# DeltaNet trunk: pair products at fixed places in the z quarters, earlier adds of a v half, and more weight buffers with a fixed load order in the memory product

## The chip, the cores and the metric

The kernel runs on one core of one Trainium2 chip. The metric is the device time of one execution in microseconds (us). Every time below is of the kernel before the change: three timed runs, and one profiled execution whose trace is quoted.

## What is computed

A decoder trunk of two layers on 256 tokens of width 2048, in fp32. Layer 0 mixes tokens with an mLSTM, layer 1 with a gated DeltaNet. Each layer then attends to 256 memory tokens and applies a squared-ReLU MLP. Keys and values of the memory are computed once, ahead of everything. Cut to what the change touches:

```python
def rms_norm(x, g):
    y = x * rsqrt(mean(x * x, -1) + EPS)
    return y * g

kv = rms_norm(mem, mem_norm_g) @ w_mem_kv              # the memory product: k_m and v_m
...
def mlstm_mixer(h, w_in, ...):                         # layer 0
    q, k, v, o, ig, fg = split(h @ w_in)
...
def gdn_mixer(h, w_in, ...):                           # layer 1
    qkv, z, bt, a = split(h @ w_in)
    q, k, v = split(silu(causal_dwconv(qkv, conv_w)))
    q = l2_norm(q) * GD_K ** -0.5                      # 16 heads of 128
    k = l2_norm(k)
    g = -exp(a_log) * softplus(a + dt_bias)            # decays, 32 heads
    gam = cumsum(g)
    A   = (k * beta) @ k.T * exp(gam_i - gam_j)        # strictly lower, by chunks of 64
    Aqk = q @ k.T * exp(gam_i - gam_j)
    ...
    return (rms_norm(o) * silu(z)) @ w_out
```

## The kernel before

**Weights.** Every product streams its fp32 weights once from memory. A unit of 1 MB comes as two halves of 512 KB, each by one DMA that SP issues (L149) into one of four `raw` buffers. ACT rounds a half to a high part (`hi`, the CAST of L169) and DVE subtracts that from the raw to get a low part (`lo`, L170). There are three hi and three lo buffers. TensorE (PE) forms a product as high by high, low by high and high by low: three matmuls. `take` hands out the next unit and begins the loads of the units after it. All engines run their instructions in order, and so does each engine's DMA queue; the order itself is laid out ahead of time by a scheduler that ranks the instructions by priority and by its own durations. `behind(a, b)` puts an instruction after another in that order, without a wait on the chip.

**The memory product.** For each of four chunks of mem, PE transposes the chunk (`mtp`, L896) and ACT and DVE split it; k_m (L438) and then v_m (L534 to L536) follow, with one unit of weights for each 512 rows. Beside v_m, `x_chunk(c)` prepares x: `load_x(c)` loads a chunk as two pieces, PE transposes them (`ltp`, L310), ACT and DVE write them as `h` (L349, L350). `load_x` holds a load back by a MEMSET of one element, which stands behind the split of a certain half (the list `splits`). All of it is loaded by SP's queue.

**The mLSTM's q, k and v.** Units f = 4 to 15 of q and k alternate with parts of v. v is formed in two halves by sums of seven products, in seven banks. When a half is complete, `keep_v` lets ACT copy the banks out (L1009), and seven additions put them together: for the second half on DVE, for the first by POOL's accumulating DMAs (L1060), one behind each f, two behind f = 11. Then come the output gate o (L450, L456) and the heads, whose first products are `sp` (L1085).

**The DeltaNet's quarters.** For each quarter c of the heads: four units of q (`gq`), four of k (`gk`), in the first quarter also the gates (`ab`, `suf`), then the z product `gz` (L534 to L536) of four units by two halves of the tokens, which makes eight slots of twelve matmuls. After a convolution (`conv`: DVE, ACT) q and k of a head are one tile `gqk`. `norms(c)` squares the four tiles on ACT (`l2sq`, L1682), sums them on PE (`l`, L1686) and forms `rk`, `nrk` and `bq` on ACT and DVE. `decays(grp)` forms the decays `gdm`: twelve small DVE instructions (L1651, L1653) from rows `grow` that POOL loads by DMA, and two Exp on ACT (L1654). `pairs(grp)` forms for two heads the products `g` on PE (L1703, L1704), scales them out of the banks as `gm` (DVE L1705 and L1707, ACT L1709) and multiplies them by the decays (`at`, L1713), which POOL stores. These are written before and behind `early_z(c)`, and the scheduler is free to place them. The small products take turns in three banks (`psum`).

Of the kernel before, what the change touches and what calls it, by code (L numbers as in the profile page):

```python
# [7 lines left out]
F32 = mybir.dt.float32  # L8
# [29 lines left out]
class Weights:  # L38


    def __init__(self, tc, ctx, ahead, bufs):
# [5 lines left out]
        self.first, self.splits, self.n_pair = 0, None, 0  # L47
# [16 lines left out]
    def after(self, load):  # L64


        self.tc.add_manual_dep(load.ins, self.last.ins.name, mybir.DependencyInfo(
            mybir.DependencyClass.NoSync, mybir.DependencyReason.DATA), reason="issue order")
        self.last = load
# [51 lines left out]
    def begin(self, place=None):  # L121
# [25 lines left out]
        for k0 in range(0, kb, hb):  # L147
            raw = self.raw.tile([P, hb, un], F32, tag="raw", name=f"raw{i}_{k0}")
            self.last = nc.sync.dma_start(raw[:, :, :n], src[k0 * P : (k0 + hb) * P, :].rearrange("(kb p) n -> p kb n", p=P))  # L149
# [27 lines left out]
    def prefetch(self, n):  # L177
        while self.done < min(len(self.plan), self.taken + n):
            for half in self.begin():

                with self.tc.high_priority(offset=self.first):
                    ins = half()
                if self.splits is not None and ins:
                    self.splits.append(ins[1])
# [11 lines left out]
def trunk(ctx: ExitStack, tc, x, mem, norm_g, mem_norm_g, w_mem_kv, w_xq, w_xo, w_up, w_down,  # L196
# [272 lines left out]
    def prod_tall(key, srcs, n_fb, evac, ahead=None, then=None, wide=False):  # L469

        for f in range(n_fb):
            hi, lo, nk, n = ws.take(key, ahead)
            a = acc(f"{key}{f}")
            for k in range(nk):
# [9 lines left out]
                m = PE.matmul(a[:, 0:T], lo[k], srcs[k][:, 0:T], start=False, stop=(k == nk - 1))  # L484
            evac(f, Bank(a, wide))
# [24 lines left out]
    def prod_tok(key, srcs, n_ch, evac, after=None, post=None, start=None, free=None, split=False):  # L510
# [37 lines left out]
        for p_ in pairs:  # L548
# [22 lines left out]
            for t in range(2):  # L571
                for i in p_:
# [4 lines left out]
                    else:  # L577
                        run(i, t)
                    done(i, t)
# [247 lines left out]
    kv = kv_stack.enter_context(tc.tile_pool(name="kv", bufs=1))  # L827
    kmT = kv.tile([P, XA_H, T], F32, name="kmT")
# [4 lines left out]
    def load(dst, src, c):  # L833
        return nc.sync.dma_start(dst[c], src[0, :, c * 512 : (c + 1) * 512].rearrange("(t p) d -> p t d", p=P))
# [50 lines left out]
    def load_x(c):  # L885

        behind(V.memset(xk[c][:1, 0, 0:1], 0.0), splits[2 * c + 5])
        for t in range(2):
            nc.sync.dma_start(xk[c][:, t, :], x[0, t * P : (t + 1) * P, c * 512 : (c + 1) * 512])

    def mem_chunk(c, other=None):
# [8 lines left out]
        for i in range(4):  # L900
            k = c * 4 + i
            chain(*split_into(mh[k], banks[i % 2][:, i // 2 * T : (i // 2 + 1) * T], cols[:, COL_MEM + k : COL_MEM + k + 1]))
            if i % 2:
                chain(*first.pop(0)())
                splits.append(last[1])
# [12 lines left out]
    splits = []  # L918
    ws.splits = splits
# [57 lines left out]
    kv_stack.close()  # L977

# [8 lines left out]
    def mlstm(sc, h, rms, before):  # L987
# [61 lines left out]
        for f in range(4, KB):  # L1049
# [7 lines left out]
            for _ in range(2 if f == 11 else 1):  # L1057
# [489 lines left out]
    def gdn(g0, lead):  # L1547
# [30 lines left out]
        def prod_v(c):  # L1578
            vts[c] = [acts.tile([P, 2, T], F32, tag=f"u{c % 2 * 2 + i}", name=f"vT{c}_{i}") for i in range(2)]
            return prod_tall("gv", h, 4, lambda f, a: conv(32 + c * 4 + f, a, vts[c][f // 2][:, f % 2, :]),  # L1580
                             wide=c not in steps)
# [13 lines left out]
        with tc.tile_pool(name="gd1", bufs=1) as sc:  # L1595
# [46 lines left out]
            def decays(grp):  # L1642
# [371 lines left out]
```

## Time and profile before

| what | value |
|---|---|
| median of 3 runs | 2815.34 us (2814.28 to 2815.68) |
| the profiled execution | 2815.06 us, of which the trace spans 2813.4 us |
| PE busy | 2778.0 us, 99% of the span |
| DVE, ACT, POOL busy | 2223.1, 1843.5, 367.8 us |
| mean granted TensorE clock | 0.995 |
| moved by DMA | 633.45 MB, mean 225 GB/s |

A wait in the profile is idle time of an engine just before an instruction, with the line that waited and the instruction that ended the wait, as far as semaphore events show it. The granted clock is the share of TensorE's full rate that it was given in a stretch; at half of it a matmul of 512 columns follows the one before by 0.43 us and not by 0.23. A timeline row reads: start, duration, engine, line, operation, output and inputs, tile, count, and in brackets the idle time ahead of it with its releaser.

### The profile page before, as it was taken

How to read it: one execution, taken by the hardware profiler on the slowest of the kernel's cores; microseconds unless marked ns; L12 is line 12 of the kernel's file. 1: busy time of each engine (PE TensorE's matmuls, PEld its weight loads, DVE VectorE, ACT ScalarE, POOL GpSimd, SP SyncE). 2: the span in 40 equal slices, each digit the busy share in tenths (PEclk: the TensorE clock that was granted, in tenths of full speed). 3: DMA queues.
4: the chain of work that ended last, by engine and by line, in shares of the span. 5: the costliest groups of instructions: out<-in, count | busy, mean ns of one | idle time of the engine just before them, and what ended most of it. 6: DMA issues, size and time to landing. Idle time of an engine off the chain costs nothing.

```text
span 2813.4 us, 42450 instructions
## 1 busy us (share of the span) xinstructions
PE 2778.0 (99%) x15552; PEld 2373.1 (84%) x15552; DVE 2223.1 (79%) x3263; ACT 1843.5 (66%) x3013; POOL 367.8 (13%) x602
## 2 busy tenths in 40 slices
PE   9999999999999999999999999999999999999998
PEld 7888888888888888887887998888888888888887
DVE  6997756788999988788776895555577789999786
ACT  6666646777778776466765554544467777778763
POOL 0110000011111110002211104231000111122100
PEclk9999999999999999999999999999999999999999
DMA  7786465689999998858877778665656899999985
GB/s 236 214 227 184 151 215 166 185 238 258 262 252 255 258 256 247 263 154 237 241 207 212 219 200 283 208 198 187 214 156 197 236 261 257 266 250 257 256 246 195
DMA packets 581488, 633.45 MB, mean 225 GB/s; under 512 B 29040, under 2 KB 431296, under 8 KB 579488
## 3 DMA queue, kind: packets, MB, share of 16 engines
q1 hardware_dynamic: 530816, 516.55, 60.2%
q0 software_dynamic: 49568, 113.10, 17.4%
q8 instruction: 122, 2.00, 0.3%
q10 hardware_dynamic: 896, 1.09, 0.1%
q14 instruction: 86, 0.70, 0.1%
HBM read 545.91 MB, written 68.22 MB: 218 GB/s over the span
## 4 chain that ended last, share of the span: by engine, by line
PE 37%; DVE 6%; DMA 4%; ACT 3%; issue 2%; POOL 0%; SPq 0%; DVEq 0%; ACTq 0%; POOLq 0%
PE up L1463 6%; PE up L1465 3%; DVE lo L170 3%; PE m L1497 2%; PE m L1498 2%; PE m L1499 2%; PE g_out L535 2%; PE g_out L536 2%; PE g_out L534 2%; DMA raw<-in_gdn_w_in 1%; PE down L535 1%; PE down L536 1%; PE down L534 1%; DVE cv L1573 1%; PE gz L534 1%
## 5 line engine op out<-in xcount | busy, mean ns | idle before, releaser
L170 DVE TENSOR_TENSOR lo<-raw,hi 128x1024 fp32r<-128x1024 f32 (+1 forms) x716 | 849.9, 1219 | 241.2 <-ACT hi L169 239.4
L169 ACT CAST hi<-raw 128x1024 fp32r<-128x1024 f32 (+1 forms) x716 | 723.4, 1048 | 354.3 <-issue 38.9
L1463 PE MATMUL up<-h,hi 128*128 128x512 f32 x1792 | 424.9, 389 | 0.9 <-ACT h_up L1291 0.9
L1463 PEld LDWEIGHTS up<-h,hi 128*128 128x128 f32 x1792 | 336.0, 188 | 72.2 <-ACT h_up L1291 2.2
L94 DVE TENSOR_TENSOR lo<-tsum,hi 128x1024 fp32r<-128x1024 f32 x208 | 247.1, 1220 | 56.5 <-ACT hi L98 40.4
L98 ACT CAST hi<-tsum 128x1024 fp32r<-128x1024 f32 x208 | 212.7, 1051 | 115.3 <-DVE tsum L94 75.2
L1465 PEld LDWEIGHTS up<-h,lo 128*128 128x128 f32 x1792 | 229.8, 191 | 8.7
L1465 PE MATMUL up<-h,lo 128*128 128x256 f32 x1792 | 232.4, 283 | 0.0
L1293 POOL DMA_DIRECT2D u<-h_up x96 | 82.8, 862 | 771.7 <-ACT h_up L1291 643.7
L94 DVE TENSOR_TENSOR lo<-rawp,hi 128x512 fp32r<-128x512 f32 (+1 forms) x160 | 150.6, 952 | 1.2 <-ACT hi L113 1.0
L1498 PE MATMUL m<-lo,s 128*128 128x512 f32 x352 | 138.5, 394 | 0.0
L1497 PE MATMUL m<-hi,s 128*128 128x512 f32 x352 | 138.4, 393 | 0.0
L1499 PE MATMUL m<-hi,s 128*128 128x512 f32 x352 | 138.1, 392 | 0.0
L1365 POOL DMA_DIRECT2D sums_d<-kept x110 | 111.0, 1111 | 147.3 <-ACT kept L1361 98.8
L535 PE MATMUL down<-lo,u 128*128 128x512 f32 x320 | 124.5, 389 | 0.0
L536 PE MATMUL down<-hi,u 128*128 128x512 f32 x320 | 124.5, 389 | 0.0
L534 PE MATMUL down<-hi,u 128*128 128x512 f32 x320 | 124.5, 389 | 0.0
L94 DVE TENSOR_TENSOR tsum<-rawp 128x1024 f32<-128x1024 f32 x80 | 97.9, 1224 | 22.4 <-DMA rawp<-in_w_down 20.6
L1573 DVE SCALAR_TENSOR_TENSOR cv<-pad,cols,cv 128x256 f32<-128x256 f32 x192 | 92.2, 481 | 16.7 <-ACT cv L1571 12.6
L1498 PE MATMUL m<-lo,u 128*128 128x512 f32 x264 | 103.9, 394 | 0.3 <-DVE lo L94 0.3
L1497 PE MATMUL m<-hi,u 128*128 128x512 f32 x264 | 103.8, 393 | 0.0
L1499 PE MATMUL m<-hi,u 128*128 128x512 f32 x264 | 103.1, 391 | 0.0
(542 smaller groups left out, 6669.4 us busy)
## 6 DMA issues: line engine op xcount, KB each, us to landing
raw<-in_w_up SPq DMA_DIRECT2D x256, 512.0 KB, 6.2
raw<-in_gdn_w_in SPq DMA_DIRECT2D x192, 512.0 KB, 5.0
rawp<-in_w_down SPq DMA_DIRECT2D x160, 512.0 KB, 6.5
raw<-in_mlstm_w_in SPq DMA_DIRECT2D x96, 512.0 KB, 4.7
raw<-in_w_down SPq DMA_DIRECT2D x96, 512.0 KB, 5.5
raw<-in_gdn_w_out SPq DMA_DIRECT2D x64, 512.0 KB, 4.8
sums_d<-kept POOLq DMA_DIRECT2D x38, 512.0 KB, 8.4
sums_d<-kept POOLq DMA_DIRECT2D x72, 256.0 KB, 7.2
```

The costliest lines, as they stand in the source:

```text
L94: sub = lambda d, a, b: nc.vector.tensor_tensor(d, a, b, ALU.subtract)
L98: nc.scalar.copy(ht[:, j : j + 2, :], t[:, j : j + 2, :])
L169: a = nc.scalar.copy(h_, raw[:, :, :n])
L170: return a, nc.vector.tensor_tensor(l_, raw[:, :, :n], h_, ALU.subtract)
L534: PE.matmul(a, sh, hi[j], start=(kk == 0), stop=False)
L535: PE.matmul(a, sh, lo[j], start=False, stop=False)
L536: end[0] = PE.matmul(a, sl, hi[j], start=False, stop=(kk == nk - 1))
L1463: PE.matmul(a, hi[k], h[k][:, :], start=(k == 0), stop=False, skip_group_check=True)
L1465: PE.matmul(a[:, T:], lo[k], h[k][:, 0:T], start=False, stop=(k == nk - 1), skip_group_check=True)
L1497: PE.matmul(a, sh, hi[i], start=(j == 0), stop=False)
L1498: PE.matmul(a, sh, lo[i], start=False, stop=False)
L1499: PE.matmul(a, sl, hi[i], start=False, stop=(j == FK // 2 - 1))
```

## The change

It has three parts.

1. **Memory product.** A second pool `wmore` of five buffers takes the halves whose running number leaves over 4 when divided by 9 (5 to 8, 14 to 17 and so on); the other halves keep the four buffers. All loads of this stage (mem, weights, x) are chained on SP in the order in which the program writes them. The MEMSETs that held the x loads back are removed. `wmore` is closed with the stage.
2. **Adds of the first v half.** `1 if f < 11 else 2`: of the seven adds one goes behind f = 10 and two each behind f = 11, 12 and 13, where before it was one behind f = 10, two behind 11, and one each behind 12 to 15.
3. **z quarters.** `norms` and `pairs` are cut into steps, and a list gives the slots of `gz` behind which a step stands. Slot 1: the first two squares. Slot 4: their sums, and the other two squares. Slot 5: their sums, with rk, nrk and bq. Slot 6: the first decays and the first pair. Slot 7: the second pair. Slot 8: the second decays and the third pair. The fourth pair stands behind the first unit of the next `gq` (or `gv`). The small matmuls are put behind the slot's last matmul, the decays on DVE behind the step before them.

```diff
@@ Weights.begin
-            raw = self.raw.tile([P, hb, un], F32, tag="raw", name=f"raw{i}_{k0}")
-            self.last = nc.sync.dma_start(raw[:, :, :n], ...)
+            self.halves += 1
+            pool = self.more if self.more and self.halves % 9 > 4 else self.raw
+            raw = pool.tile([P, hb, un], F32, tag="raw", name=f"raw{i}_{k0}")
+            d = nc.sync.dma_start(raw[:, :, :n], ...)
+            if self.more:
+                self.after(d)
+            self.last = d
@@ the memory product
+    ws.more = kv_stack.enter_context(tc.tile_pool(name="wmore", bufs=5))
...
-        return nc.sync.dma_start(dst[c], src[0, :, c * 512 : (c + 1) * 512]...)
+        ws.after(nc.sync.dma_start(dst[c], src[0, :, c * 512 : (c + 1) * 512]...))
...
-        behind(V.memset(xk[c][:1, 0, 0:1], 0.0), splits[2 * c + 5])
         for t in range(2):
-            nc.sync.dma_start(xk[c][:, t, :], ...)
+            ws.after(nc.sync.dma_start(xk[c][:, t, :], ...))
...
     kv_stack.close()
+    ws.more = None
@@ mlstm
-            for _ in range(2 if f == 11 else 1):
+            for _ in range(1 if f < 11 else 2):
@@ gdn, decays: each of the twelve
-                            V.tensor_scalar(dm[kh][:, v2, tt, :], ...)
+                            behind(V.tensor_scalar(dm[kh][:, v2, tt, :], ...), other)
@@ gdn
+            at_m, ends, l2, gdms = [], [], {}, {}
+
+            def turn(m, todo):
+                at_m[:] = [m]
+                while todo:
+                    do, *args = todo.pop(0)
+                    do(*args)
+
+            def g_mm(*a, **kw):
+                behind(PE.matmul(*a, **kw), at_m[0])
+
+            def squares_of(c, i0):
+                for i in (i0, i0 + 1):
+                    sq = l2[i] = acts.tile([P, 2, T], F32, tag=f"u{12 + i % 2}", name="l2sq")
                     S.activation(sq, qks[c][i], AF.Square)
+
+            def l2_sums(c, i0):
...
+            def decay(c, g):
+                gdms[2 * c + g] = decays(2 * c + g, ends[0]), g0.tile([P, 6, 4, P], F32, tag="at", name="at")
+
+            def pair(c, g, kh):
...
@@ early_z
-                prod_tok("gz", h, 1, ev)
+                turns = [[(squares_of, c, 0)], [], [], [(l2_sums, c, 0), (squares_of, c, 2)], [(l2_sums, c, 2)],
+                         [(decay, c, 0), (pair, c, 0, 0)], [(pair, c, 0, 1)], [(decay, c, 1), (pair, c, 1, 0)]]
+                prod_tok("gz", h, 1, ev, slot=lambda m: turn(m, turns.pop(0)))
+                later.append((pair, c, 1, 1))
...
-                norms(c)
-                pairs(c * 2)
                 early_z(c)
-                pairs(c * 2 + 1)
```

How the order moves on three engines follows, at the places of which the prediction speaks.

SP's queue near the start, before, from the fifth unit of the weights on (`raw` is a half of weights, `xs` a piece of x):

```order
L149 DMA raw_0_405<-in_w_mem_kv 128x2x512
L149 DMA raw_2_407<-in_w_mem_kv 128x2x512
L889 DMA xs_104<-in_x 128x512
L149 DMA raw_0_415<-in_w_mem_kv 128x2x512
L149 DMA raw_2_417<-in_w_mem_kv 128x2x512
L149 DMA raw_0_486<-in_w_mem_kv 128x2x512
L889 DMA xs_104<-in_x 128x512
L149 DMA raw_2_488<-in_w_mem_kv 128x2x512
L889 DMA xs_104<-in_x 128x512
L149 DMA raw_0_545<-in_w_mem_kv 128x2x512
L149 DMA raw_2_547<-in_w_mem_kv 128x2x512
```

The same stretch of the change:

```order
L152 DMA raw_0_408<-in_w_mem_kv 128x2x512
L152 DMA raw_2_410<-in_w_mem_kv 128x2x512
L152 DMA raw_0_418<-in_w_mem_kv 128x2x512
L152 DMA raw_2_420<-in_w_mem_kv 128x2x512
L897 DMA xs_104<-in_x 128x512
L897 DMA xs_105<-in_x 128x512
L152 DMA raw_0_487<-in_w_mem_kv 128x2x512
L152 DMA raw_2_489<-in_w_mem_kv 128x2x512
L897 DMA xs_104<-in_x 128x512
L897 DMA xs_105<-in_x 128x512
L152 DMA raw_0_545<-in_w_mem_kv 128x2x512
L152 DMA raw_2_547<-in_w_mem_kv 128x2x512
```

Before, four pieces of x also stood ahead of or inside the third unit of weights, and of the others some between the halves of a unit. Now the first x pieces stand behind six whole units, and from there a chunk's pieces alternate with units. `raw_0_545` is the half whose cast stands on ACT just ahead of the first `h` of x, before and now.

DVE in the first quarter, before, at the decays and the small tiles of `norms` (`bq` reads `l`):

```order
L1651 TENSOR_SCALAR gdm<-grow,cum,cml 128x128
L1653 TENSOR_SCALAR gdm<-grow,sufb 128x128
L1651 TENSOR_SCALAR gdm<-grow,cum,cml 128x128
L373 RECIPROCAL rk<-rk 128x8
L1691 TENSOR_SCALAR bq<-l_12141 128x2x4
L1690 TENSOR_SCALAR nrk<-rk 128x2x4
L1651 TENSOR_SCALAR gdm<-grow,cum,cml 128x128
L1653 TENSOR_SCALAR gdm<-grow,sufb 128x128
L1705 SCALAR_TENSOR_TENSOR gm<-g_12193,rk,masks 128x2x128
L1707 SCALAR_TENSOR_TENSOR gm<-g_12194,rk,masks 128x2x128
```

The same place in the change:

```order
L377 RECIPROCAL rk<-rk 128x8
L1715 TENSOR_SCALAR bq<-l_12215 128x2x4
L1714 TENSOR_SCALAR nrk<-rk 128x2x4
L1657 TENSOR_SCALAR gdm<-grow,cum,cml 128x128 x2
L1659 TENSOR_SCALAR gdm<-grow,sufb 128x128
L1657 TENSOR_SCALAR gdm<-grow,cum,cml 128x128
L176 TENSOR_TENSOR lo_12480<-raw_0_12475,hi_12479 128x1024
L176 TENSOR_TENSOR lo_12480<-raw_8_12477,hi_12479 128x1024
L1657 TENSOR_SCALAR gdm<-grow,cum,cml 128x128
L1659 TENSOR_SCALAR gdm<-grow,sufb 128x128
L1657 TENSOR_SCALAR gdm<-grow,cum,cml 128x128 x2
L1659 TENSOR_SCALAR gdm<-grow,sufb 128x128
```

The reciprocal, `bq` and `nrk` stood behind most decays and stand ahead of all of them now; two splits of weights have come in among the decays, and the `gm` follow three rows further on.

PE in the second quarter, before, at the first sums (`gz_0` and `gz_1` are the two halves of the tokens):

```order
L536 MATMUL gz_1_12948<-hi_12759,h_11431 128x512
L534 MATMUL gz_1_12948<-hi_12759,h_11428 128x512
L1686 MATMUL l_12867<-ones,l2sq 128x2 x4
L1703 MATMUL g_12919<-gqk_12458 128x512
L1704 MATMUL g_12920<-gqk_12458 128x256
L535 MATMUL gz_1_12948<-lo_12760,h_11428 128x512
```

PE at the first sums of that quarter in the change:

```order
L541 MATMUL gz_1_12868<-lo_12816,h_11463 128x512
L542 MATMUL gz_1_12868<-hi_12815,h_11463 128x512
L1694 MATMUL l_12941<-ones,l2sq 128x2 x8
L540 MATMUL gz_0_12867<-hi_12873,h_11597 128x512
L541 MATMUL gz_0_12867<-lo_12874,h_11597 128x512
```

Before, the first sums and the first pair stood seven matmuls into slot 2 of `gz`. Now the sums of two tiles stand behind the last matmul of slot 4, and the pair follows behind slots 5 and 6. In the first quarter PE's order hardly differs: there the small matmuls stand in the next `gq` in both, and only the later `g` stand further apart.

More of the change, by code (lines that the diff above doesn't have):

```diff
@@ L46, in __init__ @@
         self.plan, self.ready, self.ahead, self.done, self.taken = [], [], ahead, 0, 0
-        self.first, self.splits, self.n_pair = 0, None, 0
+        self.first, self.n_pair, self.more, self.halves, self.last = 0, 0, None, 0, None
     def add(self, key, w, k0, kn, n0, nn, tall=False):
@@ L64, in after @@
     def after(self, load):
-        self.tc.add_manual_dep(load.ins, self.last.ins.name, mybir.DependencyInfo(
-            mybir.DependencyClass.NoSync, mybir.DependencyReason.DATA), reason="issue order")
+        if self.last:
+            self.tc.add_manual_dep(load.ins, self.last.ins.name, mybir.DependencyInfo(
+                mybir.DependencyClass.NoSync, mybir.DependencyReason.DATA), reason="issue order")
         self.last = load
@@ L181, in prefetch @@
                 with self.tc.high_priority(offset=self.first):
-                    ins = half()
-                if self.splits is not None and ins:
-                    self.splits.append(ins[1])
+                    half()
     def take(self, key, ahead=None):
@@ L467, in prod_feat, with prod_tall @@
         return m
-    def prod_tall(key, srcs, n_fb, evac, ahead=None, then=None, wide=False):
+    def prod_tall(key, srcs, n_fb, evac, ahead=None, then=None, wide=False, slot=None):
         for f in range(n_fb):
@@ L508, in few_sums, with prod_tok @@
         return p_[:, 0 : 2 * n].rearrange("p (t n) -> p t n", t=2)
-    def prod_tok(key, srcs, n_ch, evac, after=None, post=None, start=None, free=None, split=False):
+    def prod_tok(key, srcs, n_ch, evac, after=None, post=None, start=None, free=None, split=False, slot=None):
         nk = len(srcs)
@@ L578, in prod_tok @@
                         run(i, t)
+                    if slot:
+                        slot(end[0])
                     done(i, t)
@@ L833, in load @@
     def load(dst, src, c):
[L834 removed]
+        ws.after(nc.sync.dma_start(dst[c], src[0, :, c * 512 : (c + 1) * 512].rearrange("(t p) d -> p t d", p=P)))
     def squares(rms, tok, c, after):
@@ L1640, in load_rows, with decays @@
                     rows_of[grp].append(r_)
-            def decays(grp):
+            def decays(grp, other):
                 dm = [acts.tile([P, 2, 3, P], F32, tag=f"y{grp % 2 * 2 + i}", name="gdm") for i in range(2)]
@@ L1650, in decays @@
                         for tt in range(2):
[L1651 to L1653 removed]
+                            behind(V.tensor_scalar(dm[kh][:, v2, tt, :], gr[tt][:, hh, :], cum[:, tt, hv : hv + 1],
+                                                   cml[:, tt, hv : hv + 1], ALU.min, ALU.subtract), other)
+                        behind(V.tensor_scalar(dm[kh][:, v2, 2, :], gr[1][:, hh, :], sufb[:, hv : hv + 1], None,
+                                               ALU.add), other)
                     S.activation(dm[kh], dm[kh], AF.Exp)
@@ L1668, in prod_q @@
                 if c:
-                    prod_tall("gq", h, 4, ev, wide=True)
+                    prod_tall("gq", h, 4, ev, wide=True, slot=lambda m: turn(m, later))
                 else:
@@ L1685, in norms @@
                             o_ = (((a_ * 2 + t) * 4) + i) * 2
-                            PE.matmul(sp[:, o_ : o_ + 2], sq[:, a_, t * P : (t + 1) * P], ones[:, 0:2], start=True, stop=True)
+                            g_mm(sp[:, o_ : o_ + 2], sq[:, a_, t * P : (t + 1) * P], ones[:, 0:2], start=True, stop=True)
+                if i0 == 0:
+                    return
                 sv = sp[:, 0:32].rearrange("p (a t i d) -> p a t i d", a=2, t=2, i=4)
```

70 lines of the change are left out of this document (33 added, 37 removed).

## The prediction

> **What bounds the kernel now.** I read the busy shares first, then PE's waits, then the table of stretches with the granted clock, and then the timelines around each wait. The page's first part:
>
> ```profile
> PE 2778.0 (99%) x15552; PEld 2373.1 (84%) x15552; DVE 2223.1 (79%) x3263; ACT 1843.5 (66%) x3013; POOL 367.8 (13%) x602
> ```
>
> PE is busy for 2778.0 of 2813.4 us, and the change takes no product away from it. So a gain can only come out of 35.4 us of idle time and out of stretches in which PE ran at a lower clock. PE's waits, where each is named by the waiting line and by what ended the wait (total, times, longest):
>
> ```profile
> PE sp L1085 <- ACT m L1009: 4.2, 1, 4.2
> PE l L1686 <- ACT l2sq L1682: 3.8, 2, 2.5
> PE ltp L310 <- DVE h L350: 3.6, 1, 3.6
> PE g L1703 <- ACT gdm L1654: 3.1, 1, 3.1
> PE k_m L438 <- ACT hi L169: 1.5, 2, 1.2
> PE g L1704 <- ACT gm L1709: 0.3, 1, 0.3
> ```
>
> All six lie in places that the diff touches: ltp and k_m in the memory product, sp behind the qk/v stage, l and g in the z quarters. The table by stretches (busy us and count of PE, PEld, DVE, ACT, POOL, then PE's granted clock, DMA share, GB/s) shows what followed the waits:
>
> ```profile
> 0.00:20.00 20.00, 18.17 (x107) 16.44 (x108) 9.53 (x18) 10.53 (x20) 6.03 (x21) 1.00 0.92 314
> 20.00:40.00 20.00, 18.84 (x108) 16.32 (x108) 14.09 (x25) 13.76 (x23) 0.00 (x0) 1.00 0.73 234
> 40.00:60.00 20.00, 16.37 (x69) 13.44 (x68) 12.07 (x23) 10.88 (x22) 0.00 (x0) 0.83 0.78 255
> 100.00:140.00 40.00, 40.00 (x202) 34.03 (x201) 39.80 (x55) 28.46 (x38) 3.40 (x4) 1.00 0.78 206
> 240.00:260.00 20.00, 15.81 (x101) 14.45 (x100) 13.31 (x28) 13.86 (x25) 0.00 (x0) 0.91 0.52 152
> 1280.00:1300.00 20.00, 16.89 (x89) 13.45 (x89) 15.14 (x37) 9.86 (x13) 6.11 (x11) 1.00 0.84 238
> 1320.00:1340.00 20.00, 18.62 (x92) 15.04 (x91) 19.95 (x49) 16.16 (x24) 3.35 (x10) 0.93 0.82 254
> 1340.00:1360.00 20.00, 20.00 (x99) 16.66 (x98) 9.41 (x12) 15.03 (x20) 1.51 (x4) 0.99 0.64 167
> 1420.00:1440.00 20.00, 20.00 (x92) 15.59 (x91) 15.88 (x28) 12.93 (x19) 2.64 (x6) 1.00 0.55 142
> 1480.00:1500.00 20.00, 17.54 (x81) 14.30 (x80) 13.92 (x24) 12.90 (x22) 0.40 (x4) 0.83 0.57 171
> ```
>
> After four of the waits the granted clock fell. The loss is (1 - clock) times the length: 0.09 x 20 = 1.8 us in 240:260, 0.07 x 20 + 0.01 x 20 = 1.6 us around 1340, and 3.4 us in 1480:1500 of which PE idled a little, so 3.3. Those are costs that the list of waits does not show.
>
> **The start (more weight buffers, fixed load order).** Rows of PE, ACT and SP there:
>
> ```profile
> 22.79 2.11 PE L438 MATMUL k_m<-u,hi 128*128 128x512 f32 x8 [1.16 <-ACT hi L169]
> 47.24 0.38 PE L310 MATMUL ltp<-ident,xs 128*128 128x128 f32 x2
> 51.26 1.51 PE L310 MATMUL ltp<-ident,xs 128*128 128x128 f32 x6 [3.63 <-DVE h L350]
> 57.19 0.39 PE L536 MATMUL v_m<-hi,u 128*128 128x512 f32 x1
> 46.49 1.05 ACT L169 CAST hi<-raw 128x1024 fp32r<-128x1024 f32 x1 [2.59 <-DMA raw<-in_w_mem_kv]
> 36.30 3.09 SPq L149 DMA_DIRECT2D raw<-in_w_mem_kv  x2
> ```
>
> The transposes ltp of x wait for their banks, these for h on ACT and DVE, and h stands on ACT behind a cast whose weights were issued at 36.30 and landed at about 46.4. From 51.26 to 57.19 PE then ran at half clock, so (57.19 - 51.26) / 2 = 2.9 us are lost besides. The change leaves that cast ahead of h on ACT, but brings its load earlier. In the new order 4 pieces of mem, 15 halves of weights (that one included) and 6 pieces of x are ahead or equal: 19 x 0.524 + 6 x 0.262 = 11.5 MB. At 274 GB/s, the mean of the first two stretches, the last of it lands at 42.0 us, at 314 at 36.6. The wait is gone if it lands by 46.4 - 3.6 = 42.8. I take 0.5 us of it as kept, for the banks are still handed on by ACT and DVE; the bounds are nothing kept and all of it kept. The 1.16 us wait of k_m goes in the same way, since its weights no longer queue behind pieces of x on SP. The x pieces now go behind 12 halves: 18 pieces or 9 MB, some 33 us at 274 GB/s, against their first use at 47.24. Four MEMSETs leave DVE, worth nothing there. Sum: 1.2 + 3.1 + 2.9 = **7.2** (bounds 1.2 and 7.7). It is carried on only if DVE, 39.80 of 40 us busy in 100:140, starts its splits earlier too; in 40:60 it has 7.9 us free, and PE is the one that never idles in 100:140.
>
> **The adds of the first v half.** POOL's, ACT's and PE's rows around the wait of sp:
>
> ```profile
> 211.78 1.20 POOL L1060 DMA_DIRECT2D v<-v  x1
> 237.95 1.22 POOL L1060 DMA_DIRECT2D v<-m  x1
> 240.50 0.63 ACT L1009 ACTIVATE m<-m 128x512 f32<-128x512 f32 x1
> 246.61 0.60 ACT L1009 ACTIVATE m<-m 128x512 f32<-128x512 f32 x1 [5.48 <-DMA v<-m]
> 247.26 2.06 PE L1085 MATMUL sp<-qk 128*128 128x128 f32 x12 [4.18 <-ACT m L1009]
> qk<-h_qk POOLq DMA_DIRECT2D x6, 128.0 KB, 3.0
> ```
>
> The last add of the first half leaves POOL at 237.95, ACT's next write into the buffer it reads waits for its landing until 246.6, and sp waits for the bank that ACT empties there. In the change the seventh add is issued behind f = 13, where 211.78 stands now, 26 us earlier, so that wait ends. Then ACT empties the last banks at 240.5 + 3 x 0.6 = 242.3, and PE arrives at 247.26 - 4.18 = 243.1. The other input, the last qk add, leaves POOL just ahead of 237.95 and takes 3.0 us: 241. Both are in time, by about 1 and 2 us. POOL holds two more issues of 1.2 us in gaps of some 10 us, so no qk add behind them moves. Sum: 4.2 + 1.8 = **6.0** (lower bound 4.2, if the clock falls anyway).
>
> **The z quarters.** Of the first quarter:
>
> ```profile
> 1287.56 1.10 PE L1703 MATMUL g<-gqk 128*128 128x512 f32 x2 [3.11 <-ACT gdm L1654]
> 1285.56 0.35 DVE L1651 TENSOR_SCALAR gdm<-grow,cum,cml 128x128 f32<-128x128 f32 x1 [1.30 <-DMA grow<-g_d]
> 1287.29 0.12 DVE L1691 TENSOR_SCALAR bq<-l 128x8 f32<-128x8 f32 x1
> 1287.34 1.98 ACT L169 CAST hi<-raw 128x1024 fp32r<-128x1024 f32 x2
> 1290.26 2.35 DVE L170 TENSOR_TENSOR lo<-raw,hi 128x1024 fp32r<-128x1024 f32 x2
> ```
>
> There are three banks. The third g takes that of l, which bq empties at 1287.4; bq waits on DVE behind decays that wait for a row by DMA until 1285.56, and PE follows at 1287.56. (The releaser that the view names is not the last.) In the new DVE order bq stands ahead of the decays, so this wait goes. But the gm that empty the first pair's banks now stand behind all twelve decays and two splits, and the fourth g, 29 products later, needs such a bank. At 16.89 / 89 = 0.19 us each (1280:1300) that is 5.5 us, so PE comes at 1287.56 - 3.11 + 5.5 = 1290.0. DVE would be through at 1285.8 + 2.35 + 8 decays (1.8) + 2 gm (0.8) = 1290.8; if the casts of those splits come as late as here, ending at 1289.3, at 1289.3 + 1.2 + 1.8 + 0.8 = 1293.1. So 0.8 to 3.1 us of waiting return; I take 2.0, the middle, as both rows bear on it. Gain 3.4 - 2.0 = 1.4 (3.4 is the 3.1 and the 0.3 of the list).
>
> Of the second quarter, and the wait in the fourth:
>
> ```profile
> 1329.98 0.39 PE L534 MATMUL gz<-hi,h 128*128 128x512 f32 x1
> 1334.10 0.39 PE L534 MATMUL gz<-hi,h 128*128 128x512 f32 x1
> 1335.87 1.05 PE L1686 MATMUL l<-ones,l2sq 128*128 128x2 f32 x8 [1.38 <-ACT l2sq L1682]
> 1335.19 0.63 ACT L1682 ACTIVATE l2sq<-gqk 128x512 f32<-128x512 f32 x1
> 1339.68 0.42 ACT L1574 ACTIVATE gqk<-cv 128x256 f32<-128x256 f32 x1
> 1487.63 1.87 PE L1686 MATMUL l<-ones,l2sq 128*128 128x2 f32 x8 [2.46 <-ACT l2sq L1682]
> ```
>
> A gz product takes (1334.10 - 1329.98) / 18 = 0.229 us, a slot of twelve 2.75. The sums of the first two squares now stand behind slot 4, at 1329.98 + 11.0 = 1341.0, where that square is ready at 1335.8. In the fourth quarter l stands ahead of gz now, so there it moves by 11 us against 2.46. Both waits go, and with them 1.6 and 3.3 us of clock. What is late next: the other two squares use the buffers of the first two, so ACT takes them once the first sums are read, at 1342.0, and needs 2 x 0.63: 1343.3, or 1345.2 with two casts ahead; slot 5 ends at 1344.7. The last conv is ready at 1340.1 and does not decide. From 1.4 us to spare to 0.5 late: I take 0.2. A pair's g at a fixed slot may wait for the pair before it: from nothing (the third quarter shows no such wait, 20.00 of 20 us in 1420:1440) to 2.35, if two splits come in between on DVE; I take 0.6 a quarter, twice the 0.3 of g L1704. So each of the last three quarters pays 0.8: gains of 1.4 + 1.6 - 0.8 = 2.2, of -0.8, and of 2.5 + 3.3 - 0.8 = 5.0. With the first, **7.8** (upper bound 12.2, all that the quarters lose now).
>
> **Sum.** 7.2 + 6.0 + 7.8 = 21.0 us. The profiled execution took 2815.06 us, 0.3 under the median of 2815.34, so the forecast is 2815.06 - 21.0 = 2794.1.
>
> [...]
>
> **The rivals.** First, the start gives only its 1.2: the load lands no earlier, for it is the queue's rate that sets it (234 GB/s in 20:40), or the shift is used up by DVE in 100:140. Against it: the buffers, not the rate, held the loads, since 0:20 ran at 314. Time 2794.1 + 6.0 = 2800.1.
>
> Second, the clock in the z quarters falls as before, since small products and short waits at the sums are enough for it: 4.9 us stay, 2799.0. For it: it fell after only 1.38 us. Against it: the third quarter has the same small products, no wait, and a clock of 1.00.
>
> Third, on the other side: the fixed slots come too early for ACT and DVE in every quarter. The sums of slot 5 and the first pair behind slot 6 each wait as long as the longest wait at l now, 2.5 us, and the clock falls as in the fourth quarter, 3.3: 8.3 a quarter, 33.2 in all. Then 2815.06 - 7.2 - 6.0 - 12.2 + 33.2 = 2822.9, slower. It decides from (25.4 + 5.6) / 4 = 7.75 us a quarter on. Against it: the margins above, which are 1 us and not -2.5.
>
> Fourth, first and second together with the bad ends of the quarters (3.1 - 2.0 = 1.1 in the first; 2.35 - 0.6 and 0.5 - 0.2, so 2.05, in each of three): 21.0 - 6.0 - 4.9 - 1.1 - 6.2 = 2.8 us are left, 2812.3, which is no change that can be told.
>
> **How the numbers follow.** 0.2%, or 5.6 us, is about what can be told from no change. Chances: the forecast 0.52, the first rival 0.18, the second 0.20, the third 0.04, the fourth 0.06. So faster 0.90, within 0.06, slower 0.04. The low end is everything gained, 7.7 + 6.0 + 12.2 = 25.9, so 2789.2, less 0.8 for the fastest run shown: 2788. The high end takes the first two rivals together, 2794.1 + 6.0 + 4.9 = 2805.0, and 3 us, less than half, of the bad ends: 2808.
>
> **What would show it.** Right: the ltp and sp waits under 1 us, a clock of 1.00 in the stretches that now have 0.83, 0.91, 0.93 and 0.83, a wait of 1 to 4 us at g in the first z quarter and under 1 us at l and g elsewhere. Wrong at the start if the cast ahead of h still begins after 43 us; wrong in the quarters if l of slot 5 waits over 1 us or the clock there is under 1.00.

## The result

The changed kernel takes 2794.47 us, the median of six runs (2790.01 to 2798.35). The kernel before took 2811.55 us in the six runs beside it (2807.57 to 2815.68). The ratio on record is 0.9947, with a 95% interval of 0.9933 to 0.9961: 14.9 us less, or 10.9 to 18.8 (the two medians alone differ by 17.1). In a second set of runs the ratio was 0.9946 (0.9930 to 0.9963). The time lies 0.4 us from the forecast of 2794.1 us and inside the range of 2788 to 2808. But the forecast subtracted 21.0 us from an execution of 2815.06 us; the sets of runs of the kernel before have medians of 2809.9 to 2811.6 us and reach from 2801 to 2821. So the time was met far closer than the gain, which is partly luck, and the experiments had to say which terms were real.

The profiled execution after spans 2794.4 us against 2813.4. PE's waits in the same view as before (waiting line, releaser, total, times, longest; `...` marks lines left out, here and in all that follows):

```profile
PE up L1469 <- ACT h_up L1297: 2.8, 2, 1.5
PE xo L540 <- ACT u L351: 2.3, 2, 1.4
...
PE sp L1091 <- ACT dm L1109: 1.2, 1, 1.2
...
PE ltp L314 <- DVE h L354: 0.7, 1, 0.7
...
PE k_m L442 <- ACT hi L175: 0.4, 1, 0.4
```

The waits at `l` and `g` are not in the list any more; `ltp` fell from 3.6 to 0.7 and `sp` from 4.2 to 1.2. The longest are now `up` and `xo`, products of the MLPs and of the attention, where no part changes a line: 2.8 and 2.3 us, against 0.9 and 0.6 in the trace of before. In the traces of the parts alone they are as long, 1.8 to 3.1 and 2.3 to 3.1, so it was the trace of before that had them short. The stretches that answer to those shown of before (busy us and count of PE, PEld, DVE, ACT, POOL; granted clock, DMA share, GB/s):

```profile
20.00:40.00 20.00, 20.00 (x119) 17.57 (x117) 15.97 (x22) 13.58 (x24) 0.00 (x0) 1.00 0.83 289
40.00:60.00 20.00, 19.33 (x99) 16.09 (x98) 15.34 (x32) 16.41 (x35) 0.00 (x0) 1.00 0.62 201
...
240.00:260.00 20.00, 18.83 (x131) 17.50 (x132) 14.48 (x46) 14.53 (x32) 0.00 (x0) 1.00 0.51 159
...
1260.00:1280.00 20.00, 19.88 (x99) 16.16 (x99) 7.70 (x21) 10.03 (x13) 4.68 (x7) 0.83 0.68 188
...
1320.00:1340.00 20.00, 20.00 (x107) 17.05 (x106) 15.25 (x31) 13.30 (x23) 0.40 (x4) 1.00 0.72 202
...
1480.00:1500.00 20.00, 20.00 (x101) 16.22 (x100) 13.16 (x28) 14.73 (x18) 0.67 (x2) 1.00 0.75 197
```

The clock is 1.00 where it was 0.83, 0.91, 0.93 and 0.83, and 0.83 in a place where it was not: 1260:1280, in the first z quarter, where PE waited for almost nothing (19.88 of 20 us busy). Along the program the two traces part as follows. q starts at 60.29 and not 67.71 (7.4 us), the first products of the heads' values (`np`), behind `sp`, 11.3 us earlier, the DeltaNet's first gq at 1184.83 and not 1194.50 (9.7), the end 19.0 us earlier.

Three rows on ACT and POOL of the changed kernel show the two mechanisms at the start and at `sp`:

```profile
41.12 1.05 ACT L175 CAST hi<-raw 128x1024 fp32r<-128x1024 f32 x1 [3.87 <-DMA raw<-in_w_mem_kv]
42.07 0.83 ACT L353 ACTIVATE h<-ltp,cols 128x256 fp32r<-128x256 f32 x2
```

```profile
206.95 1.74 POOL L1066 DMA_DIRECT2D v<-m  x2 [2.15 <-DMA v<-v]
```

The cast ahead of `h` begins at 41.1 and not 46.5: its weights landed inside the 36.6 to 42.0 us that the prediction had worked out. The last two adds of the v half leave POOL at 207, where the last one left at 237.95.

### The profile page after: what moved, and what is told of

Its sections match the earlier page's. It is cut to its first block, busy times and chain, and to the rows that moved or that the text cites. A ratio compares the mean times of both kernels' runs of the same rounds, so it can differ in the third digit from the quotient of the medians.

```text
span 2794.4 us, 42444 instructions
## 1 busy us (share of the span) xinstructions
PE 2771.5 (99%) x15552; PEld 2369.8 (85%) x15552; DVE 2223.2 (80%) x3259; ACT 1835.0 (66%) x3006; POOL 368.1 (13%) x602
## 4 chain that ended last, share of the span: by engine, by line
PE 85%; DVE 5%; DMA 5%; ACT 3%; issue 1%; SPq 0%; POOL 0%; DVEq 0%; ACTq 0%; POOLq 0%
PE up L1469 13%; PE up L1471 7%; PE m L1504 5%; PE m L1503 5%; PE m L1505 5%; PE down L541 3%; PE down L542 3%; PE down L540 3%; PE gv L480 2%; PE gk L480 2%; PE gz L540 2%; PE o L454 2%; PE gz L542 2%; PE gz L541 2%; PE g_out L541 2%; PE g_out L540 2%
## 5 line engine op out<-in xcount | busy, mean ns | idle before, releaser
L540 PE MATMUL gz<-hi,h 128*128 128x512 f32 x256 | 104.2, 407 | 0.0
L1503 PE MATMUL m<-hi,u 128*128 128x512 f32 x264 | 103.9, 394 | 0.0
```

Of the source, the lines that this page charges most:

```text
L540: PE.matmul(a, sh, hi[j], start=(kk == 0), stop=False)
L1503: PE.matmul(a, sh, hi[i], start=(j == 0), stop=False)
```

## The experiments

Theory 1, as the runs below call it: the three parts are separate gains, and, as an assumption, a stretch falls to half clock when the one before it held too little work for the array (in the trace of before, PE waited or ran matmuls of two columns for 0.62 to 0.77 of the 3.41 us ahead of each of four falls). The rivals: the start's gain is given back later, the quarters' gain is chance of the clock, or the parts overlap.

### Each part alone, and the whole again

Each part's lines of the diff alone, on the kernel before (shortened to the lines that say most):

```diff
 e1_start: part 1
+            pool = self.more if self.more and self.halves % 9 > 4 else self.raw
+            if self.more:
+                self.after(d)
-        behind(V.memset(xk[c][:1, 0, 0:1], 0.0), splits[2 * c + 5])
 e2_adds: part 2
-            for _ in range(2 if f == 11 else 1):
+            for _ in range(1 if f < 11 else 2):
 e3_quarters: part 3
-                norms(c)
-                pairs(c * 2)
                 early_z(c)
-                pairs(c * 2 + 1)
+                prod_tok("gz", h, 1, ev, slot=lambda m: turn(m, turns.pop(0)))
 e4_all: the changed kernel as it is
```

Expected of part 1: 

> Only part 1 (buffers and load order of the memory product) is put on the kernel before. Theory 1, three separate gains: q starts 7 us earlier than in the kernel before (the whole change shows 67.71 -> 60.29), the wait of sp at about 241 stays near 4 us with its half clock, the waits in the z quarters stay, and the time falls by 7 us (5 to 9). Rival, the start is given back: the busy DVE of 60 to 240 us takes the gain, q is early but o starts less than 3 us earlier than 237.82, and the time falls by less than 3 us.

Expected of part 2: 

> Only part 2 (the adds of the first v half) is put on the kernel before. Theory 1: the 4.2 us wait of sp is replaced by one of about 1.2 us, behind ACT's table load, at the second sp (as the trace of the whole change shows), and the half clock at 248 goes: 4.2 + 1.8 - 1.2 = 4.8 us less. Rival, the ACT chain behind sp is as late without the adds: the time falls by under 2 us.

Expected of part 3: 

> Only part 3 (fixed places in the z quarters) is put on the kernel before. Theory 1: no wait of PE over 0.3 us in the z quarters, the half clock at the second and fourth quarter goes, and the time falls by 8 to 11 us, less 1.7 or 3.4 us where small products in the first quarter bring the clock down. Rival, the quarters' gain in the trace is chance of the clock and not the waits: the time falls by under 4 us, with half clock in two or more quarters.

Expected of the whole: 

> The whole change again, beside its parts on one chip. Theory 1: the differences of the three parts add up to this one's within 3 us, some 19 us less than the kernel before. Rival, the parts overlap: this one gains over 4 us less than their sum.

The last column is the ratio's distance from 1 times 2810.91 us.

| kernel | median us | ratio to before (2810.91) | 95% interval | less than before |
|---|---|---|---|---|
| part 1 alone | 2810.30 | 0.9994 | 0.9982 to 1.0006 | 1.7 us (-1.7 to 5.1) |
| part 2 alone | 2807.02 | 0.9986 | 0.9973 to 0.9999 | 3.9 us (0.3 to 7.6) |
| part 3 alone | 2801.24 | 0.9961 | 0.9948 to 0.9974 | 11.0 us (7.3 to 14.6) |
| all | 2796.46 | 0.9946 | 0.9930 to 0.9963 | 15.2 us (10.4 to 19.7) |

The parts add up: 1.7 + 3.9 + 11.0 = 16.6 against 15.2, within the 3 us of theory 1. An overlap of a few us could hide in intervals of about 3.5 us to either side. The whole is 15.2 and not "some 19". Part 3 gave what theory 1 had, but not without a wait: its trace has one of 0.95 us in the first quarter. Part 2 gave 3.9 where 4.8 was expected; the interval still includes the rival's "under 2", and it is the trace that speaks for theory 1 (`sp` waits 1.0 us, the clock is 1.00 in 240:260). Part 1 failed: it gives under 5.1 us and perhaps nothing, not 7. In its trace q starts at 59.80 and the first `np` behind `sp` at 253.61, 7.9 and 7.5 us ahead of the trace of before, but the end is only 3.3 us ahead: the clock fell and PE waited in later places, which part 1 does not touch (0.91 in 1020:1040 and 1720:1740, where it was 1.00 before; 6.2 us at `up` and `xo`, and 1.5 before). And the trace of before was late: other traces without part 1 start q at 62.16 to 64.49. PE's waits with part 1 alone:

```profile
PE sp L1087 <- ACT m L1011: 3.8, 1, 3.8
...
PE l L1688 <- ACT l2sq L1684: 2.6, 3, 1.1
...
PE g L1705 <- ACT gdm L1656: 1.7, 1, 1.7
```

With part 2 alone, and then with part 3 alone, the start being that of the kernel before in both:

```profile
PE ltp L310 <- DVE h L350: 1.9, 1, 1.9
...
PE sp L1085 <- ACT dm L1103: 1.0, 1, 1.0
```

```profile
PE ltp L310 <- DVE h L350: 2.0, 1, 2.0
...
PE k_m L438 <- ACT hi L169: 1.7, 2, 1.4
```

With part 1 `ltp` is not among the waits of its trace that reach 0.6 us. But without it the wait is 1.9 and 2.0 us here, not 3.6, and the clock did not fall behind it: q started at 62.16 and 63.53 and not at 67.71. The `k_m` wait, too, is 1.7 us in one of the two and 0.3 in the other, where before it was 1.5. The execution on which the prediction was built had the longest of these waits.

### The start by itself

To see the start without the scatter of the 2,400 us behind it, four kernels end behind the mLSTM's heads and leave out all that follows. The cut, and what each has of part 1:

```diff
 all four, and the two further down
                 y, post = mlstm(sc, h0, xrms, x_rest)
+                for f in range(KB):
+                    o_ = t256("cut")
+                    V.tensor_copy(o_, y[f][:, 0:T])
+                    nc.sync.dma_start(o_v[:, :, f * P : (f + 1) * P], ...)
+            ts_stack.close()
+            return
 t0_cut_before: nothing else; t1_cut_start: part 1
 t2_cut_order: part 1, but all halves from the four old buffers
+            pool = self.raw
 t3_cut_pool: the kernel before, and only the buffers of part 1
+            pool = self.more if self.more and self.halves % 9 > 4 else self.raw
```

Expected of the cut kernel before: 

> The kernel before, ended behind the mLSTM's heads: 16 tiles of its result are copied out as they are, and all that follows (the output product, attention, MLPs, layer 1) is left out. It is the measure for the three kernels beside it, with less behind the start that can vary. Theory 1: waits at k_m of 1.2 to 1.4 us and at ltp of 1.9 to 3.6 us, as the traces of the full kernels without part 1 show, sp waits about 4 us. Rival: without what follows nothing at the start changes, so there is none for this run.

Expected with part 1: 

> Part 1 on the kernel that is ended behind the mLSTM's heads (the rest left out, as in the kernel it is compared with). Theory 1: the two waits at the start go, the clock stays at 1.00 more often, nothing is given back, and it takes 3 to 7 us less than the same kernel without part 1. Rival, given back: DVE between 60 and 240 us or the wait of sp takes it, and it takes under 1.5 us less.

Expected with the order alone: 

> Of part 1 only the fixed load order and the missing MEMSETs, with the four old buffers, on the kernel ended behind the mLSTM's heads (the rest left out). Theory 1, the buffers hold the loads: the k_m wait goes, since the weights stand ahead of x, but the half ahead of h lands after 43 us and ltp still waits 1 to 4 us; it takes at least 2 us more than the one with all of part 1. Rival, the order alone does it: within 1 us of that.

Expected with the buffers alone: 

> Of part 1 only the five more buffers, with the loads ordered by the scheduler and the MEMSETs kept, on the kernel ended behind the mLSTM's heads (the rest left out). In SP's queue the first half of the seventh unit then stands behind weights of the mLSTM. Theory 1: PE waits at v_m for that unit, over 3 us, and it takes longer than the kernel without part 1. Rival, the buffers alone do it: it takes as little as the one with all of part 1, within 1 us.

| kernel | runs | median us | lowest to highest | q starts at |
|---|---|---|---|---|
| as before | 4 | 369.34 | 367.70 to 371.04 | 63.97 |
| part 1 | 4 | 368.71 | 368.28 to 369.63 | 60.21 |
| order alone | 4 | 370.76 | 369.51 to 370.99 | 63.45 |
| buffers alone | 5 | 369.47 | 367.26 to 370.45 | 60.23 |

Part 1 brings q forward by 3.8 us and the time by 0.6, within the scatter of these runs. Here most of the gain was given back, as the rival said. Of the 3.8 us, 2.8 are left where o starts (230.95 against 233.77) and 1.7 at the first `np` (253.28 against 255.02). The second loss lies at `sp`, whose waits show it. The `sp` waits as before and with part 1:

```profile
241.19 1.60 PE L1085 MATMUL sp<-qk 128*128 128x128 f32 x12 [2.16 <-ACT m L1009]
246.38 1.60 PE L1085 MATMUL sp<-qk 128*128 128x128 f32 x12 [1.29 <-ACT dm L1103]
```

```profile
239.44 2.93 PE L1087 MATMUL sp<-qk 128*128 128x128 f32 x12 [3.23 <-ACT m L1011]
```

With part 1 PE reaches `sp` earlier, waits 3.23 us for the add instead of 2.16, which is the 1.1 us lost there. The twelve products then take 2.93 us instead of 1.60: the clock had fallen behind this wait and not behind the other. That fall costs little here, for in the kernel before PE waits 1.29 us for ACT at the next `sp`, and with part 1 it does not. The table of stretches of the kernel with part 1 has it:

```profile
220.00:240.00 20.00, 16.77 (x91) 14.38 (x90) 15.56 (x21) 11.19 (x17) 1.77 (x2) 0.97 0.84 244
240.00:260.00 20.00, 20.00 (x135) 18.51 (x134) 16.25 (x46) 16.75 (x32) 0.00 (x0) 0.94 0.47 149
```

The order alone does not bring the load forward (the cast ahead of `h` begins at 43.89, and q at 63.45; it takes 2.0 us more than all of part 1, as expected): the buffers hold the loads. The buffers alone do: q starts at 60.23, and the time is within 1 us of part 1's, as it is of the kernel before. My expectation that a half behind the mLSTM's weights would make PE wait fell; there was no wait at `v_m`. The rates suggest why, first with part 1, then with the buffers alone:

```profile
20.00:40.00 20.00, 20.00 (x115) 17.42 (x114) 16.41 (x24) 14.28 (x24) 0.00 (x0) 1.00 0.78 276
```

```profile
20.00:40.00 20.00, 20.00 (x115) 17.40 (x114) 15.92 (x26) 14.25 (x24) 0.00 (x0) 1.00 1.05 386
40.00:60.00 20.00, 20.00 (x107) 16.96 (x106) 15.92 (x34) 16.41 (x35) 0.00 (x0) 1.00 0.37 104
```

With the buffers alone the loads ran at 386 GB/s, and little was left for the next 20 us (104 GB/s), so a half far back in the queue still came in time. Why the fixed order ran at 276 with the same buffers was not tried. Nor is a rate by itself a sign of the buffers: the traces with the four old ones ran at 200 to 274 GB/s in 20:40. So of what part 1 does to q the buffers do the work, and the fixed order adds nothing that shows; no time in this table is clear of the first row.

Since the gain was lost at `sp`, it should come through where part 2 has taken that wait away:

```diff
 t4_cut_adds: the cut, and part 2; t5_cut_both: the cut, part 1 and part 2
+            for _ in range(1 if f < 11 else 2):
```

Expected of part 2: 

> Part 2 alone on the kernel ended behind the mLSTM's heads (the rest left out). Theory 1: the wait of sp for the accumulating DMA goes (2.2 to 4.2 us), one of 1.3 us behind the table load stays, and it takes 2 to 4 us less than the same kernel without part 2, whose median is 369.34. Rival, what is late behind it takes the gain: under 1 us less.

Expected of both: 

> Parts 1 and 2 on the kernel ended behind the mLSTM's heads (the rest left out). Theory 1, the gain of part 1 is lost in the wait of sp while that wait is there, and carries through once part 2 has taken it away: 3 to 5 us less than part 2 alone. Rival, part 1 is worth nothing with or without that wait: within 1 us of part 2 alone.

Part 2 took 366.20 us (365.91 to 369.38), 3.1 less than the cut kernel before by the medians, as expected; but the two ranges overlap, and they are of two sets of runs. Both took 364.94 (364.22 to 365.29): 1.3 less by the medians, and its longest run is below the shortest with part 2 alone. That lies between the two theories: part 1 is worth more than nothing once `sp` no longer waits, and less than the 3 to 5 us I had expected. The waits of the kernel with both:

```profile
PE sp L1087 <- ACT dm L1105: 1.3, 1, 1.3
PE k_m L442 <- ACT hi L175: 0.6, 1, 0.6
```

The profiled executions of these two differ by 4.7 us (spans 367.7 and 363.0) where the medians differ by 1.3; that of part 2 alone was the longest of its four, so the 4.7 is the less typical of the two. Where the rest of q's lead goes stays open.

### What brings the clock down

The half clock of 1260:1280 stood in both traces of the whole change, with no wait ahead of it. In the trace shown it lasted from 1271.3 to 1278.2. What precedes it there are sums of squares, matmuls of two columns:

```profile
1268.24 1.95 PE L1694 MATMUL l<-ones,l2sq 128*128 128x2 f32 x16
1270.05 0.36 PE L481 MATMUL gq<-h,lo 128*128 128x256 f32 x1
...
1270.95 0.39 PE L480 MATMUL gq<-h,hi 128*128 128x512 f32 x1
1271.17 1.55 PE L1694 MATMUL l<-ones,l2sq 128*128 128x2 f32 x8
1272.58 0.56 PE L481 MATMUL gq<-h,lo 128*128 128x256 f32 x1
1272.94 0.63 PE L480 MATMUL gq<-h,hi 128*128 128x512 f32 x1
```

Two experiments, on the changed kernel: the sums of the last three quarters twice, and the sums spread out (both shortened).

```diff
 e5_twice
+                            for _ in range(2 if c else 1):
                                 g_mm(sp[:, o_ : o_ + 2], sq[...], ones[:, 0:2], start=True, stop=True)
 e6_spread
-                turns = [[(squares_of, c, 0)], [], [], [(l2_sums, c, 0), (squares_of, c, 2)], [(l2_sums, c, 2)],
-                         [(decay, c, 0), (pair, c, 0, 0)], [(pair, c, 0, 1)], [(decay, c, 1), (pair, c, 1, 0)]]
+                turns = [[(squares_of, c, 0, 1)], [], [], [(l2_sums, c, 0), (squares_of, c, 2)],
+                         [(l2_sums, c, 1), (squares_of, c, 3)], [(l2_sums, c, 2)], [(l2_sums, c, 3)],
+                         [(decay, c, 0), (pair, c, 0, 0)]]
+                rest = [[(pair, c, 0, 1)], [], [(decay, c, 1), (pair, c, 1, 0)], [], [(pair, c, 1, 1)]]
+                if c == 0:     # sum of tile 0 behind slot 8, the others behind half units of the next gq
```

Expected of the doubled sums: 

> The whole change, in which the sums of squares of the second to fourth z quarter are issued twice, into the same places with the same result: 16 more matmuls of two columns a quarter, 3.6 us each quarter at full clock, 10.8 in all, and no more waiting. Theory 1, a stretch of 3.41 us falls to half clock when over about half of the one before it holds no work of the array, and matmuls of two columns are none: half clock after the sums in all three quarters, and 16 to 21 us more than the whole change. Rival, only idle time of PE counts: the clock stays 1.00 there and it takes 11 us more.

Expected of the spread sums: 

> The whole change with the sums of one tile of squares at a time, a slot of 2.75 us apart (before two at a time), in the first quarter in half units of the next gq; the pairs move back into the next gq. Theory 1: the half clock in the first z quarter, which both traces of the whole change show, goes, no window there is idle by over 0.45, and it takes 1.7 to 3.4 us less than the whole change. Rival, the pairs in gq wait for banks as the first quarter's did before, and the gain is lost: within 1 us of the whole change, or slower.

With the sums doubled the time is 2815.87 us (ratio to before 1.0024, 1.0009 to 1.0039), 19.4 us over the whole change of the second set by the medians and 21.9 by the two ratios: the upper end of what theory 1 had, and not the rival's 11. In its trace 27.3 us ran at half clock ahead of the kernel's last 20 us, against 6.8 in either trace of the whole change. That is 10.2 us more lost, beside the 10.8 of the sums; 1.7 of these lie in the first quarter, whose sums were not doubled. The third quarter shows it. Its doubled sums, then gz with 0.43 us from one matmul to the next; and stretches of the second, third and fourth quarter, without any idle time:

```profile
1410.56 3.63 PE L1694 MATMUL l<-ones,l2sq 128*128 128x2 f32 x32
1418.21 2.12 PE L1694 MATMUL l<-ones,l2sq 128*128 128x2 f32 x16
```

```profile
1416.08 0.63 PE L541 MATMUL gz<-lo,h 128*128 128x512 f32 x1
1416.51 0.63 PE L542 MATMUL gz<-hi,h 128*128 128x512 f32 x1
```

```profile
1320.00:1340.00 20.00, 20.00 (x115) 17.43 (x114) 14.28 (x25) 13.26 (x22) 0.40 (x4) 1.00 0.73 208
1340.00:1360.00 20.00, 20.00 (x99) 15.74 (x97) 13.56 (x30) 13.62 (x16) 2.80 (x5) 1.00 0.54 148
1400.00:1420.00 20.00, 20.00 (x107) 17.25 (x105) 10.55 (x15) 10.89 (x16) 0.30 (x3) 0.91 0.68 188
1420.00:1440.00 20.00, 20.00 (x90) 15.78 (x91) 11.37 (x26) 13.09 (x15) 2.24 (x4) 0.91 0.40 114
...
1500.00:1520.00 20.00, 20.00 (x86) 15.77 (x85) 7.66 (x22) 9.88 (x11) 0.57 (x1) 0.81 0.27 76
```

PE is busy for 20.00 of 20 us and the clock is 0.91, 0.91 and 0.81. In one point the expectation failed: the second quarter kept a clock of 1.00 with the same doubled sums (1320:1360). So the same work brings the clock down in one place and not in another. Cut into stretches of 3.41 us, as the last section does, the second quarter's sums filled 0.45 to 0.57 of four stretches in a row; in the third quarter they filled 0.6 and 0.9 of the two ahead of the falls.

With the sums spread, the first quarter keeps its clock:

```profile
1260.00:1280.00 20.00, 19.81 (x119) 16.68 (x118) 10.60 (x24) 11.81 (x16) 4.68 (x7) 1.00 0.79 215
```

From the first gq (1187.83) to the late gz behind the last gv (1688.99) it takes 501.2 us, against 505.9 and 504.3 in the two traces of the whole change. The time is 2793.11 us (2791.92 to 2796.67), with the ratio to before of the whole change, 0.9946 (0.9925 to 0.9967): 3.4 and 1.4 us under its two medians, which is the size expected and not more than such runs scatter. In the first quarter of this trace no stretch of 3.41 us is idle or in such sums by more than 0.26, under the 0.45 expected, and `g` waits nowhere, so the rival's banks did not hold it. So the trace agrees with theory 1, and the time neither bears it out nor denies it. One trace is thin: with part 3 alone the first quarter kept its clock too, with the sums not spread, and took 503.4 us between the same two points.

## Why the prediction was right, and where it was not

The direction, the time and the places were right. The sizes of the terms were not: measured alone they are 1.7, 3.9 and 11.0 us where 7.2, 6.0 and 7.8 were forecast. Two were too large and one too small, and the sum of 21.0, outside the measured 10.9 to 18.8, was taken from an execution 3.5 to 5 us slower than the medians of 2809.9 to 2811.6. That the time came out within 0.4 us is luck in that much.

**The start, 7.2 us forecast.** The mechanism held: the load came at 41 us, the waits of `k_m` and `ltp` fell to 0.4 and 0.7, and in the profile q moved by 7.4. The step that failed is "Sum: 1.2 + 3.1 + 2.9 = **7.2**": it priced one execution's wait, and the clock's fall behind it, as if every execution had them. In the five traces without part 1 the `ltp` wait was 3.6 (before), 1.9 and 2.0 (parts 2 and 3 alone), 2.4 and 2.9 us (the cut kernels before and with part 2), and the clock fell behind it in the first and the last two (0.83 in 40:60 before, 0.91 in the cut kernel before). The `k_m` wait, priced at 1.2, was 1.5 to 1.7 us in two of the five and 0.3 to 0.5 in the others. Measured: 1.7 us (-1.7 to 5.1) alone, 0.6 and 1.3 by the medians of the cut kernels. My first rival, at 0.18 "the start gives only its 1.2", is nearer to this than the forecast, though by another mechanism: the load did land earlier. In the cut kernels about 1 us of the 3.8 at q was lost by the start of o and 1.1 in a longer wait at `sp`; with part 1 alone on the whole kernel o started 8.0 us earlier than in the trace of before, so there nothing had been lost up to o, and DVE had not taken it.

**The adds, 6.0 us forecast.** The add no longer holds `sp`. In the two profiles PE reaches `sp` 6.87 us earlier and the first `np` behind it 11.34: 4.5 us. Part 2 alone gave 3.9 (0.3 to 7.6), the cut kernel 3.1. "Both are in time" held at the first `sp`, where PE no longer waits. The step that failed is "Sum: 4.2 + 1.8 = **6.0**": it asked what is late at the first `sp` and not at the second, where ACT now comes late through a table load. PE's row, then ACT's, of the changed kernel:

```profile
241.17 1.60 PE L1091 MATMUL sp<-qk 128*128 128x128 f32 x12 [1.18 <-ACT dm L1109]
```

```profile
238.94 1.28 ACT L1109 ACT_TABLE_LOAD   x1
240.23 0.88 ACT L1109 ACTIVATE dm<-ep,mg 128x128 f32<-128x128 f32 x3
```

Before, the same load stood on ACT behind the 4.2 us wait:

```profile
250.21 1.28 ACT L1103 ACT_TABLE_LOAD   x1
```

PE did not wait for it then, for it ran at half clock from 248.24 to 251.65 and came late itself. The cut kernel before, whose clock stayed at 1.00 there, has both waits, 2.16 and 1.29 us. So the half clock lay over a wait that comes back without it, and 6.0 - 1.2 = 4.8 was the term.

**The z quarters, 7.8 us forecast.** Part 3 alone measured 11.0 (7.3 to 14.6). By quarter, from one gk to the next in the two profiles: 0.2 us in the first (forecast 1.4), 3.4 in the second (2.2), 0.3 in the third (-0.8), 4.9 in the fourth, up to the late gz (5.0): 8.8. In the trace of part 3 alone, whose clock did not fall there, it is 2.3, 3.8, 0.3 and 4.8: 11.2, close to the 11.0 of its runs. The waits that I had put at the fixed slots, 0.8 a quarter, did not come: in the second to fourth of the new quarters no trace has a wait at `l` or `g`. In the first quarter the step "So 0.8 to 3.1 us of waiting return" did not hold for the whole change. DVE emptied the bank at 1282.3, about as late as worked out once the 9.7 us are allowed for by which all of it is earlier, but PE came later, at 1283.5, because the clock had fallen (half clock from 1271.3 to 1278.2), which the prediction had named as a sign of being wrong:

```profile
1276.78 1.71 PE L1694 MATMUL g<-gqk 128*128 128x512 f32 x2
1283.50 0.59 PE L1694 MATMUL g<-gqk 128*128 128x256 f32 x2
```

So a loss of clock took the place of the wait. With part 3 alone the clock did not fall there (1.00 in 1260:1300), and the wait stands where it was forecast, at the fourth g and behind gm, at the low end of its range:

```profile
1288.71 0.70 PE L1692 MATMUL g<-gqk 128*128 128x256 f32 x2 [0.95 <-DVE gm L1732]
```

A further gain I had not seen: the DeltaNet's products behind the quarters, also called `np`, waited 1.8, 3.0 and 2.5 us for a DMA in the three traces of whole kernels with the old quarters, and not at all in the five with the new ones. With parts 1 and 2 alone the clock fell behind it as well, to 0.91 in 1720:1740, another 1.7 us. With part 1 alone the row was

```profile
PE np L1858 <- DMA tn<-tn_d: 3.0, 2, 1.6
```

Why the new quarters are ahead of that DMA was not tried.

**The clock.** The second rival, half clock in the quarters without a wait, was right about the first quarter of the whole change (0.83 in 1260:1280) and wrong about the others (1.00 in 1320:1340 and 1480:1500). The length of a wait did not decide the falls: before, the clock fell after 1.38 us (0.93 in 1320:1340) and not after 3.11 (1.00 in 1280:1300). Nor did a fall need a wait: the doubled sums brought the clock to 0.91 and 0.81 with PE busy for 20.00 of 20 us. Of the windows counted in the last section those ahead of a fall were idle by 0.30 to 0.91, none as a whole.

**The third rival**, slots that come too early, did not happen: in the five traces with the new quarters `l` waits nowhere, and `g` once, for the 0.95 us shown.

## What to carry to other kernels

Price a wait from several executions before you add what hangs on it: the same wait was 1.9 to 3.6 us here, and the clock's fall behind it came in three traces of five. Ask what is late next at every place where the chain meets the same queue again, not only at the first. And count the clock in the work as well as in the waits: behind a bunch of matmuls of two columns the products ran at half clock in the third quarter of the doubled sums (0.91 in 1420:1440), though not in the second (1.00 in 1320:1360). Spreading the bunch kept the clock in the one trace of it (1.00 in 1260:1280); the time did not show it.

## What the runs showed of the hardware

In the eight traces of full kernels, ahead of the last 20 us, half clock came in stretches of 3.4 us or twice that. In the trace of before these begin at 50.27, 248.24, 1337.09 and 1487.28 us, whose distances are 58, 319 and 44 times 3.413, so they lie on one grid. I cut the eight traces of full kernels into such windows and counted as idle the time in which PE waited or ran matmuls of two columns. Most windows ahead of a fall were idle by 0.54 to 0.91 (0.62 to 0.77 in the trace of before); two of about 0.30, which also held ten short passes of `suf` (six over 32 columns, four over 128 from weights of 32), were followed by half clock as well. Of the windows behind which the clock stayed, the highest had 0.57. A short matmul is counted here up to the start of the next one; other ways move these shares by up to 0.05. So windows idle by 0.54 to 0.57 stand on both sides, and where a limit lies these runs do not say; that the short passes of `suf` count as idle in part would explain the two of 0.30, and was not tried. A wait of 3.11 us, which left the clock alone, lay across two windows, 1.43 us in one and 1.68 in the other, 0.42 and 0.49 of them; one of 1.38 with 1.05 us of sums, which brought it down, lay in one.

Behind a window at half clock, less idle time went with another one: of such windows in these traces, the seven that were idle by 0.21 to 0.61 were followed by half clock again, and the 23 idle by at most 0.17 by full clock. With a second window a fall cost 3.4 us (half of 6.83) and not 1.7.

The same kernel also scattered by more than I had expected: 2801 to 2821 us before, where the first three runs lay within 1.4 us of each other. The grid lies differently in each of the eight traces, by 0.18 to 2.89 us from the span's start. That the same short waits therefore cost half clock in some executions and not in others, and that this makes the scatter, is a guess and was not shown.
